# The MLP's up projections as seven products, weights standing and 256 tokens moving, with the norm's weight applied to turned tokens

## The chip, the cores and the metric

One of the eight cores of a Trainium2 chip. The metric is device time of one execution, in microseconds (us). Before the change three runs took 983.56 to 983.86 us, median 983.71.

## What is computed

One layer of a decoder trunk on 512 tokens of 1024 numbers, all in float32. A token mixer (retention and dilated attention, left out here) is added to x, then an MLP, then a gated embedding. The change lies in the MLP's first product and what feeds it and takes from it:

```python
def rmsnorm(x, g):
    y = x * rsqrt(mean(x * x, axis=-1) + EPS)
    return y * g

    x = x + (gate_r * ret_branch + gate_a * att_branch) @ w_o   # w_o: 1024 x 1024
    u = rmsnorm(x, g_mlp) @ w_up                                # w_up: 1024 x 4096
    x = x + square(relu(u)) @ w_down                            # w_down: 4096 x 1024
    gate_p = sigmoid(rmsnorm(x, g_ple) @ w_ple_gate)
    return x + gate_p * (p_i @ w_ple_proj)
```

## The kernel before

**Splits and passes.** TensorE multiplies rounded numbers, so each operand is held as a high part (a rounded copy, by ScalarE, ACT) and a low part (the difference, by VectorE, DVE). A product is three matmul passes into one bank (`mm3`, L256 to L261): high by high, high by low, low by high. A pass has one tile of 128 x 128 standing in TensorE and up to 512 columns moving through it.

**Weights.** They come in units of 512 KB in the order of a plan written ahead. `fetch` has SyncE (SP) load a unit into one of six `raw` tiles; where the plan asks for a sum of two blocks, a second transfer adds to the tile while it lands, issued by GpSimd (POOL, L211 and L225). `ahead` splits units, two or three of them in advance of their use (`AHEAD`); `split_unit` makes the high part on ACT (L247) and the low part on DVE (L248), in one step of 128 x 1024 each, into one of four pairs of tiles (whi, wlo). Where a norm's weight is to be applied, it does so in four steps of 128 x 256 on each engine (L252, L253), the weight of the input channel as a factor.

**Seven products.** `seven_gemm` multiplies 512 x 512 quarters of a matrix by Strassen's scheme in Winograd's form: seven block products instead of eight. The weights' factors are quarters B11, B21, B22 and sums T1 to T4; the left factors are seven blocks of 256 tokens, and each result is added with a sign to one or two quarters of the output (L1120, one step for each half of the tokens and each quarter). `SEVEN` is the order of the products by halves of their inner length. The result banks come from two pools of four; the table `BANK` says which products share one.

**The tail.** `tail` runs, in this order: the output projection (`seven_gemm` on w_o); the embedding product, whose result waits in memory; four groups of the MLP (index f), each an up group (1024 columns of w_up) and a down group (1024 rows of w_down); the gate's product and the sum.

An up group is eight column tiles of `cols_gemm`: weights stand, 512 tokens move, 24 passes a tile. Its input h2 is x turned (tokens to columns) and split by `gain_T`; the norm's weight g_mlp is applied to w_up at the split of its units, and the norm's factor of each token is applied after the MLP's square (f2). `act` takes each finished tile: relu and square on ACT, then, as soon as a pair of quarters is there, `seven_left` builds the differences on DVE and `left_split` the high and low parts of the down group's left factors (L1084 on ACT, L1085 on DVE, up to six blocks of 256 in one step). The down group is a `seven_gemm` that adds into x.

**Order.** Each engine runs its instructions in a fixed order. A scheduler sets it from the program's order and its own estimates; in the stage of the output projection and in the last group's down part, the order on ACT and DVE is the one written in the program (`manual_schedule`), and there `later` and `force` put steps some ticks (a tick is a few matmuls) behind.

Of the kernel before, what the change touches and what calls it, by code (L numbers as in the profile page):

```python
# [11 lines left out]
F32 = mybir.dt.float32  # L12
# [24 lines left out]
FACTOR = {1: "B11", 2: "B21", 3: "B22", 4: "T4", 5: "T1", 6: "T2", 7: "T3"}  # L37
SEVEN_UNITS = [(FACTOR[m], v) for m, u in SEVEN for v in ((0, 1) if u is None else (u,))]
LEFT = {1: 0, 2: 1, 4: 2, 7: 3, 5: 4, 6: 5, 3: 6}
# [41 lines left out]
class Block:  # L81
# [86 lines left out]

    def plan_seven(self, w, r0, c1, c2, vector=False):
# [4 lines left out]
        at = lambda name, u: n + SEVEN_UNITS.index((name, u))  # L174
        for name, u in SEVEN_UNITS:
            if name == "T1":
                src = q(0, 1, u) if vector else (q(0, 1, u), q(0, 0, u))
                if vector:
                    self.added[at("B11", u)] = at("T1", u), at("B11", u)
            elif name == "T4" and vector:  # L180
# [111 lines left out]
    def stat(self, act, k, t, perm):  # L292
        out = []
        for part in act:
            c = part[k // 4][:, k % 4]
            out.append(R(c.rearrange("p (l r) -> p r l", r=DIL)[:, t] if perm else c[:, t * P : (t + 1) * P]))
        return out
# [204 lines left out]
    def embed_load(self):  # L502
        self.pT = self.big("pT")
        self.p_raw = self.big("praw")[:, 0:2]
        self.nc.sync.dma_start(self.p_raw, self.a["p_cols"].rearrange("(k p) t -> p k t", p=P))

    def embed_split(self):
        nc, pT, raw = self.nc, self.pT, self.p_raw
        hi, lo = pT[:, 0:2], pT[:, 2:4]
        nc.scalar.activation(R(hi), raw, AF.Copy)  # L510
        nc.vector.tensor_tensor(R(lo), raw, hi, op=ALU.subtract)

    def embed(self):
        nc = self.nc
        hi, lo = self.pT[:, 0:2], self.pT[:, 2:4]
        self.pp_dram = self.dram.tile([S, D], F32, name="pp_dram", tag="pp_dram")
        for half in range(2):
# [4 lines left out]

            self.rows_gemm(([hi], [lo]), 2, store)

# [561 lines left out]

    def seven_products(self, left, after):

        banks, begun = {}, set()
        for m, half in SEVEN:  # L1090
            us = self.units(2 if half is None else 1)
            for p, u in [(p, u) for p in range(2) for u in ((0, 1) if half is None else (half,))]:
# [3 lines left out]
                wh, wl = us[u if half is None else 0]  # L1096
                for k in range(2):
                    sh, sl = left(m, 2 * u + k, p)
                    self.mm3(banks[b], sh, sl, wh[:, k], wl[:, k], u == 0 and k == 0 and b not in begun,
                             u == 1 and k == 1, b in begun)  # L1100
                if u == 1:
# [3 lines left out]

    def seven_gemm(self, U, xs, f, ready):

        nc = self.nc

        def left(m, kk, p):  # L1110
            c = slice(LEFT[m] * 256 + p * P, LEFT[m] * 256 + (p + 1) * P)
            return (R(U[i][kk].rearrange("p a b -> p (a b)")[:, c]) for i in range(2))

# [9 lines left out]

        self.seven_products(left, after)


    def tail(self, mx):
# [3 lines left out]
        self.embed_load()  # L1131
        h2 = []
        v2 = self.const.tile([P, NT], F32, name="v2")
# [5 lines left out]
        nc.gpsimd.memset(one[:, NT:], -1.0)  # L1139
        left = [2] * NT  # L1140

        def ready(t, j):
            if not h2:
                h2.extend(self.new_act(2, "h2"))
            self.gain_T(xs[t], t, j, h2, "h2", 3)
            left[t] -= 1
            if not left[t]:
                self.mean_squares(xs[t], 7, lambda mean: (mean(v2[:, t : t + 1]), self.done.add(("v2", t))))
            if (t, j) == (3, 0):
                self.embed_split()  # L1150

        with self.tc.manual_schedule(engines={nc.scalar.engine, nc.vector.engine}):
            self.AHEAD = 3
            self.seven_gemm(mx, xs, one, ready)
            self.embed()
            for t in range(NT):
                self.force(("v2", t))
            nc.vector.reciprocal(f2[:, :NT], v2)
            nc.vector.tensor_scalar(f2[:, NT:], f2[:, :NT], -1.0, None, op0=ALU.mult)

        h3 = None
        for f in range(NF // 2):
            U = [[None] * 4, [None] * 4]
            Z = {}

            def act(b, j, ps):
                r = self.tmp("ur")
                nc.scalar.activation(r, ps, AF.Relu)
                if b == 0:
                    z = self.big("z").rearrange("p a (b t) -> p (a b) t", b=2)  # L1170
                    a21 = self.tmp("a21")[:, :256]
                    Z[j] = z, a21
                    nc.scalar.activation(z[:, 0], r[:, :256], AF.Square)
                    nc.scalar.activation(a21, r[:, 256:], AF.Square)
                    self.left_split(z, U, j, 0, 1)
                else:
                    z, a21 = Z[j]
                    nc.scalar.activation(z[:, 1:3], r.rearrange("p (h t) -> p h t", h=2), AF.Square)
                    self.seven_left(z, a21, U, j)
# [23 lines left out]
            self.seven_gemm(U, xs, f2, ready)  # L1203

# [20 lines left out]
    def make_plan(self):  # L1225
# [7 lines left out]
        for c in (0, 512):  # L1233
            self.plan_seven(w, 0, RV + c, RG + c, True)
        self.plan_mix()
        self.plan_seven(a["w_o"][0], 0, 512, 0)
        for half in range(2):
            self.plan_rows(a["w_ple_proj"][0], 512 * half, 2)
        for f in range(NF // 2):
            for jj in range(2):  # L1240
                for b in range(2):
# [46 lines left out]
```

## Time and profile before

| | |
|---|---|
| median of three runs | 983.71 us |
| the profiled execution's own time | 983.3 us |
| its span, first to last instruction | 981.2 us |
| TensorE matmuls (PE), busy | 973.4 us, 99% |
| TensorE weight loads (PEld) | 817.3 us, 83% |
| VectorE (DVE) | 649.7 us, 66% |
| ScalarE (ACT) | 492.5 us, 50% |
| GpSimd (POOL) | 110.8 us, 11% |
| TensorE clock granted | 1.000 of full speed |
| moved by DMA | 136.49 MB |

A row of a timeline gives the start in us from the span's start, the length, the engine, the line, the operation, out<-in by the program's names, and the tile's shape; "x2" at its end means that two instructions were recorded as one row. Matmuls are pipelined, so their recorded lengths overlap: what a pass costs is read from start to start, or from the length of a stretch by its count of passes. A row of busy time by stretch gives the stretch, its length, and then for each engine busy time and count. The table of DMA issues gives queue, count, KB each and the median us from issue to landing. The chain that ended last is followed back from the last instruction, at each step to what released it.

### The profile page before, as it was taken

Reading aid. Unit: us, or ns where it says so; the run is one execution under the profiler, and the core shown is the slowest. Engines: PE = TensorE matmul, PEld = TensorE weight load, DVE = VectorE, ACT = ScalarE, POOL = GpSimd, SP = SyncE. Lnnn points to the kernel's source line nnn. Section 1 sums busy time; section 2 is a strip of 40 time slices with the busy share of each in tenths; the row PEclk is TensorE's granted clock in tenths of the full one; section 3 lists DMA queues with packets and bytes.
Section 4 is the critical chain, followed back from the end, with each engine's and each line's share of the span. In section 5 each row is a group of like instructions: output and inputs, shape, how many; then the busy total and the mean of one; then the engine's idle time right before and its main releaser. Section 6 shows DMA issues by size and latency. Waiting matters only on the chain.

```text
span 981.2 us, 12477 instructions
## 1 busy us (share of the span) xinstructions
PE 973.4 (99%) x4540; PEld 817.3 (83%) x4540; DVE 649.7 (66%) x1029; ACT 492.5 (50%) x1019; POOL 110.8 (11%) x108
## 2 busy tenths in 40 slices
PE   9999999999999999999999999999999999999998
PEld 6888899889888878888888888888888888888886
DVE  7857675775969869464633875677567567667753
ACT  6535344446645547353323457654664564565551
POOL 0310120220001120001001110020001002002000
PEclk9999999999999999999999999999999999999999
DMA  9822123334247744223535676567548548555811
GB/s 333 268 86 88 44 86 86 93 125 140 79 128 186 192 112 143 67 66 108 191 91 127 147 172 215 150 121 203 149 113 209 151 108 183 166 144 119 258 63 53
DMA packets 88508, 136.49 MB, mean 139 GB/s; under 512 B 6096, under 2 KB 40576, under 8 KB 88448
## 3 DMA queue, kind: packets, MB, share of 16 engines
q1 hardware_dynamic: 75248, 110.52, 35.1%
q0 software_dynamic: 13056, 25.17, 15.7%
q8 instruction: 35, 0.57, 0.2%
q14 instruction: 25, 0.20, 0.1%
q10 hardware_dynamic: 144, 0.02, 0.0%
HBM read 131.46 MB, written 4.24 MB: 138 GB/s over the span
## 4 chain that ended last, share of the span: by engine, by line
PE 97%; DVE 1%; POOL 1%; ACT 0%; DMA 0%; issue 0%; SPq 0%; ACTq 0%
PE pg L259 29%; PE pg L261 29%; PE pg L260 29%; PE po L724 1%; PE ph L577 1%; PE pa L261 1%; PE pa L259 1%; PE pa L260 1%; PE pt L335 1%; PE sc L701 1%; PE pe L669 1%; PE kv L972 1%; PE sc L707 1%; PE ry L984 1%; POOL r L325 0%; DVE wlo L248 0%
## 5 line engine op out<-in xcount | busy, mean ns | idle before, releaser
L248 DVE TENSOR_TENSOR wlo<-raw,whi 128x1024 fp32r<-128x1024 f32 (+1 forms) x178 | 210.5, 1190 | 101.7 <-ACT whi L247 100.7
L247 ACT ACTIVATE whi<-raw 128x1024 fp32r<-128x1024 f32 (+1 forms) x177 | 182.2, 1035 | 186.6 <-PE pg L261 99.1
L259 PE MATMUL pg<-whi,hh 128*128 128x512 f32 x344 | 137.8, 402 | 0.0
L261 PE MATMUL pg<-whi,hl 128*128 128x512 f32 x344 | 134.7, 391 | 0.0
L260 PE MATMUL pg<-wlo,hh 128*128 128x512 f32 x344 | 134.5, 391 | 0.0
L259 PE MATMUL pg<-h2h,whi 128*128 128x512 f32 x256 | 99.6, 389 | 0.0
L260 PE MATMUL pg<-h2l,whi 128*128 128x512 f32 x256 | 99.6, 389 | 0.0
L261 PE MATMUL pg<-h2h,wlo 128*128 128x512 f32 x256 | 99.6, 389 | 0.0
L259 PE MATMUL pg<-whi,uh 128*128 128x512 f32 x240 | 94.2, 393 | 0.0
L261 PE MATMUL pg<-whi,ul 128*128 128x512 f32 x240 | 93.4, 390 | 0.0
L260 PE MATMUL pg<-wlo,uh 128*128 128x512 f32 x240 | 93.4, 389 | 0.0
L261 PEld LDWEIGHTS pg<-whi,hl 128*128 128x128 f32 x344 | 72.4, 210 | 11.1
L259 PEld LDWEIGHTS pg<-whi,hh 128*128 128x128 f32 x344 | 72.4, 211 | 10.5 <-ACT whi L247 0.3
L260 PEld LDWEIGHTS pg<-wlo,hh 128*128 128x128 f32 x344 | 72.6, 211 | 10.0
L252 ACT ACTIVATE whi<-raw,gcol 128x256 fp32r<-128x256 f32 (+1 forms) x144 | 65.8, 523 | 30.1 <-PE pg L261 15.4
L253 DVE SCALAR_TENSOR_TENSOR wlo<-raw,gcol,whi 128x256 fp32r<-128x256 f32 (+1 forms) x144 | 66.2, 510 | 21.5 <-ACT whi L252 21.0
L259 PE MATMUL pg<-hh,whi 128*128 128x512 f32 x160 | 64.0, 400 | 0.0
L261 PE MATMUL pg<-hh,wlo 128*128 128x512 f32 x160 | 62.4, 390 | 0.0
L260 PE MATMUL pg<-hl,whi 128*128 128x512 f32 x160 | 62.4, 390 | 0.0
L1085 DVE TENSOR_TENSOR ul<-z,uh 128x256 fp32r<-128x256 f32 (+1 forms) x40 | 43.2, 1090 | 28.3 <-ACT uh L1084 27.7
L260 PEld LDWEIGHTS pg<-h2l,whi 128*128 128x128 f32 x256 | 48.0, 188 | 10.0
L261 PEld LDWEIGHTS pg<-h2h,wlo 128*128 128x128 f32 x256 | 48.0, 188 | 10.0
(222 smaller groups left out, 1760.1 us busy)
## 6 DMA issues: line engine op xcount, KB each, us to landing
raw<-in_w_in SPq DMA_DIRECT2D x72, 512.0 KB, 3.9
raw<-in_w_up SPq DMA_DIRECT2D x32, 512.0 KB, 4.4
raw<-in_w_down SPq DMA_DIRECT2D x32, 512.0 KB, 3.4
raw<-in_w_down POOLq DMA_DIRECT2D x32, 512.0 KB, 5.8
x<-in_x SPq DMA_DIRECT2D x8, 512.0 KB, 6.7
raw<-in_w_in POOLq DMA_DIRECT2D x8, 512.0 KB, 6.4
raw<-in_w_ret_out SPq DMA_DIRECT2D x8, 512.0 KB, 3.6
raw<-in_w_o SPq DMA_DIRECT2D x8, 512.0 KB, 3.3
```

What stands on the lines that cost most here:

```text
L247: self.pin(nc.scalar.activation(R(hi[:, i]), raw[:, i], AF.Copy))
L248: nc.vector.tensor_tensor(R(lo[:, i]), raw[:, i], hi[:, i], op=ALU.subtract)
L252: self.pin(nc.scalar.activation(R(hi[:, i]), raw[:, i], AF.Copy, scale=g))
L253: nc.vector.scalar_tensor_tensor(R(lo[:, i]), raw[:, i], g, hi[:, i], op0=ALU.mult, op1=ALU.subtract)
L259: t.matmul(ps, sh, mh, start=first, stop=False, skip_group_check=more)
L260: t.matmul(ps, sh, ml, start=False, stop=False, skip_group_check=more)
L261: t.matmul(ps, sl, mh, start=False, stop=last, skip_group_check=more)
L335: nc.tensor.transpose(ps[:, k * P : (k + 1) * P], part[:, k * P : (k + 1) * P], self.ident)
L577: self.nc.tensor.transpose(ps[:, t * P : (t + 1) * P], rots[t][:, h * HD : (h + 1) * HD], self.ident)
L669: self.nc.tensor.transpose(ps[:, k * P : (k + 1) * P], e[:, k * P : (k + 1) * P], self.ident)
L701: nc.tensor.matmul(sc[:, h * P : (h + 1) * P], qT[:, h, rs], kT[:, h, rs], start=True, stop=True)
L1085: self.nc.vector.tensor_tensor(R(lo), src, hi, op=ALU.subtract)
```

## The change

Four things change, all in the tail.

1. An up group is computed by `up_products`: seven products here too, with weights standing and 256 tokens moving (`seven_products` with `turned`). For each unit of 256 x 512 weights, four column tiles of 128 by two rows of k by three passes move 256 tokens. The result banks of products 3, 5 and 1, 2 (c and b) are taken at the group's start. The units come from `plan_seven`: T1 by a DVE addition, T2, T3 and T4 by adding transfers.
2. The order of the products is `HALVES` in the up and down groups: both halves of product 1, then both of product 5. The w_o stage keeps `SEVEN`.
3. g_mlp is applied to tokens: `turn` turns a block of x by TensorE and multiplies it by g_mlp on its way out of the bank (DVE), and `quarter` builds the seven left factors of the up groups from it: four differences, seven splits of 128 x 1024.
4. The left factors are tiles by product (`slots`: high and low part of one factor in one tile) in place of tiles by rows of k; the steps that make the down group's factors are in `after`, 512 wide. The embedding's input moves to smaller tiles.

```diff
+HALVES = ((1, 0), (1, 1), (5, 0), (5, 1)) + SEVEN[4:]
...
+    def turn(self, x, out, goff):
+        ps = self.bank("pt")
+        for k in range(4):
+            self.nc.tensor.transpose(ps[:, k * P : (k + 1) * P], x[:, k * P : (k + 1) * P], self.ident)
+        g = self.gcol[:, goff : goff + 4].unsqueeze(2).to_broadcast([P, 4, P])
+        self.nc.vector.tensor_tensor(out, ps.rearrange("p (k t) -> p k t", k=4), g, op=ALU.mult)
...
-    def seven_products(self, left, after):
+    def seven_products(self, left, after, order=SEVEN, turned=False):
         banks, begun = {}, set()
-        for m, half in SEVEN:
+        if turned:
+            banks = {(x, p): self.gbank() for x in "cb" for p in range(2)}
+        for m, half in order:
...
+                for n, k in [(n, k) for n in range(2 if turned else 1) for k in range(2)]:
+                    first, last, more = u == 0 and n == 0 and k == 0 and b not in begun, u == 1 and k == 1, b in begun
+                    if turned:
+                        c = slice(256 * p + P * n, 256 * p + P * (n + 1))
+                        self.mm3(banks[b][:, 256 * n : 256 * (n + 1)], wh[:, k, c], wl[:, k, c], *left(m, 2 * u + k),
+                                 first, last, True)
+                    else:
+                        self.mm3(banks[b], *left(m, 2 * u + k, p), wh[:, k], wl[:, k], first, last, more)
...
+    def slots(self):
+        out = {}
+        def split(m, src, k):
+            if m not in out:
+                out[m] = self.big("f").rearrange("p (s k) (h t) -> p s (k h) t", s=2, h=2)
+            hi, lo = out[m][:, 0, k], out[m][:, 1, k]
+            self.nc.scalar.activation(R(hi), src, AF.Copy)
+            self.nc.vector.tensor_tensor(R(lo), src, hi, op=ALU.subtract)
+        return out, split
...
+        def after(m, p, ps):
+            k = slice(2 * p, 2 * p + 2)
+            if m in (1, 3, 5):
+                held[m, p] = self.tmp("r") if m != 5 else self.tabp.tile([P, 512], F32, tag="tab", name=self.nm("r5"))
+                nc.scalar.activation(held[m, p], ps, AF.Copy)
+                return
+            x = self.tmp("r4") if m == 4 else held[{2: 1, 6: 3, 7: 5}[m], p]
+            if m == 4:
+                nc.scalar.activation(x, ps, AF.Relu)
+            else:
+                nc.vector.tensor_tensor(x, x, ps, op=ALU.add)
+                nc.scalar.activation(x, x, AF.Relu, scale=1.0 if m == 2 else -1.0)
+            nc.scalar.activation(x, x, AF.Square)
+            if m in (2, 6):
+                split({2: 2, 6: 1}[m], v(x), k)
+                return
+            a11, a12, a21 = held[3, p], held[1, p], held[5, p]
+            if m == 7:
+                nc.vector.tensor_tensor(a11, a11, x, op=ALU.subtract)
+                split(7, v(a11), k)
+                return
+            held[4, p] = x
+            nc.vector.tensor_tensor(a21, x, a21, op=ALU.subtract)
+            split(5, v(a21), k)
+            self.differ(a11, x, a11)
+            self.differ(a12, a12, a11)
+            if p:
+                for f, n in ((3, 1), (6, 3), (4, 4)):
+                    for i in range(2):
+                        split(f, v(held[n, i]), slice(2 * i, 2 * i + 2))
...
+        def quarter(i, j):
+            if not i:
+                split(1 + j, zq[0][:, j], every)
+            elif not j:
+                nc.vector.tensor_tensor(a11, a11, a21, op=ALU.subtract)
+                split(7, a11, every)
+            else:
+                nc.vector.tensor_tensor(a21, a22, a21, op=ALU.subtract)
+                split(5, a21, every)
+                self.differ(a11, a22, a11)
+                self.differ(a12, a12, a11)
+                for m, z in ((3, a12), (6, a11), (4, a22)):
+                    self.later(0, lambda m=m, z=z: split(m, z, every), ("h2", m))
...
-            for jj in range(2):
-                for b in range(2):
-                    self.cols_gemm(h2, KD, lambda n, ps: act(b, 2 * jj + n, ps))
+            U = self.up_products(h2)
...
-                    self.plan_cols(a["w_up"][0], 512 * (2 * f + b) + 256 * jj, KD, g0=40)
-            self.plan_seven(a["w_down"][0], 1024 * f, 512, 0)
+            self.plan_seven(a["w_up"][0], 0, 1024 * f + 512, 1024 * f, HALVES, ("T1",))
+            self.plan_seven(a["w_down"][0], 1024 * f, 512, 0, HALVES)
```

The changed file has other line numbers: the split of a unit is L248 (ACT) and L249 (DVE), the three passes L260 to L262, the addition into x L1132, the factors' high and low parts L1146 and L1147, the copies of products 1, 3, 5 L1165, relu and square of products 2, 6, 7 L1172 and L1173 (of product 4, L1169 and L1173).

Three places where the order moves, all in the second group (index 1), from its up group to its down group. First ACT, before the change, from the relu of an up tile to the splits of the down group's first units (ur: relu'd tile; z: squares and differences; uh: high part of left factors; whi: high part of a weight unit):

```order
L1174 ACTIVATE a_6224<-ur_6221 128x256
L1084 ACTIVATE uh_6227<-z_6223 128x256
L1168 ACTIVATE ur_6271<-pg_6231 128x512
L1178 ACTIVATE z_6189<-ur_6271 128x512
L247 ACTIVATE whi_6313<-raw_6311 128x1024
L1084 ACTIVATE uh_6193<-z_6189 128x1536
L247 ACTIVATE whi_6334<-raw_6331 128x1024
L1168 ACTIVATE ur_6303<-pg_6232 128x512
L1178 ACTIVATE z_6223<-ur_6303 128x512
L247 ACTIVATE whi_6355<-raw_6353 128x1024
L1084 ACTIVATE uh_6227<-z_6223 128x1536
L247 ACTIVATE whi_6375<-raw_6373 128x1024
```

ACT after the change, at the end of the up group; ahead of this piece stand the split of T4's first half (whi_6436) and one relu, and its last row is the split of T4's second half (r: a tile of products, taken to relu and square in place; f: a left factor):

```order
L1172 ACTIVATE r_6326<-r_6326 128x512
L1173 ACTIVATE r_6312<-r_6312 128x512
L1173 ACTIVATE r_6326<-r_6326 128x512
L1146 ACTIVATE f_6377<-r_6312 128x512
L1146 ACTIVATE f_6377<-r_6326 128x512
L1172 ACTIVATE r_6152<-r_6152 128x512
L1172 ACTIVATE r_6166<-r_6166 128x512
L1173 ACTIVATE r_6152<-r_6152 128x512
L1173 ACTIVATE r_6166<-r_6166 128x512
L1146 ACTIVATE f_6416<-r_6152 128x512
L1146 ACTIVATE f_6416<-r_6166 128x512
L248 ACTIVATE whi_6440<-raw_6073 128x1024
```

Weight splits stood between any two or three steps of the factors; now twelve steps of the factors (the relu ahead included) stand between two weight splits.

DVE before, at the same hand-over, with the low parts of the down group's third, fourth and fifth units (wlo_6314, wlo_6335, wlo_6356, for products 1, 5 and 2) among the factors' steps:

```order
L248 TENSOR_TENSOR wlo_6314<-raw_6311,whi_6313 128x1024
L1085 TENSOR_TENSOR ul_6194<-z_6189,uh_6193 128x1536
L248 TENSOR_TENSOR wlo_6335<-raw_6331,whi_6334 128x1024
L1072 TENSOR_TENSOR z_6223<-z_6223,a_6224 128x512
L1074 SCALAR_TENSOR_TENSOR z_6223<-z_6223 128x256 x2
L248 TENSOR_TENSOR wlo_6356<-raw_6353,whi_6355 128x1024
L1085 TENSOR_TENSOR ul_6228<-z_6223,uh_6227 128x1536
L1120 SCALAR_TENSOR_TENSOR x_4534<-pg_6317,f_4842,x_4534 128x512
L248 TENSOR_TENSOR wlo_6376<-raw_6373,whi_6375 128x1024
L1120 SCALAR_TENSOR_TENSOR x_4534<-pg_6324,f_4842,x_4534 128x512
```

DVE now, the end of the same stretch; wlo_6644 is the low part of the down group's fifth unit (B21, for product 2):

```order
L1147 TENSOR_TENSOR f_6582<-r_6152,f_6582 128x512
L1147 TENSOR_TENSOR f_6545<-r_6231,f_6545 128x512
L1152 SCALAR_TENSOR_TENSOR r_6166<-r_6166,r_6326 128x512
L1147 TENSOR_TENSOR f_6587<-r_6312,f_6587 128x512
L1147 TENSOR_TENSOR f_6587<-r_6326,f_6587 128x512
L1147 TENSOR_TENSOR f_6582<-r_6166,f_6582 128x512
L1147 TENSOR_TENSOR f_6592<-r_6541,f_6592 128x512
L1147 TENSOR_TENSOR f_6592<-r_6574,f_6592 128x512
L1132 SCALAR_TENSOR_TENSOR x_4534<-pg_6605,f_4843,x_4534 128x512
L1132 SCALAR_TENSOR_TENSOR x_4534<-pg_6612,f_4843,x_4534 128x512
L249 TENSOR_TENSOR wlo_6644<-raw_6641,whi_6643 128x1024
L249 TENSOR_TENSOR wlo_6664<-raw_6661,whi_6663 128x1024
```

The fifth unit's low part now stands behind all the factors' low parts and behind the first two additions into x.

TensorE before, where the down group's product 2 begins (unit 6355 and its low part 6356, bank pa):

```order
L259 MATMUL pa_6401<-whi_6355,uh_6009 128x512
L260 MATMUL pa_6401<-wlo_6356,uh_6009 128x512
L261 MATMUL pa_6401<-whi_6355,ul_6010 128x512
L259 MATMUL pa_6401<-whi_6355,uh_6043 128x512
L260 MATMUL pa_6401<-wlo_6356,uh_6043 128x512
```

TensorE now, at the same place (f_6416 is product 2's left factor, whi_6643 and wlo_6644 its unit; f_6587 and whi_6703 belong to a product with a bank of pool pg):

```order
L260 MATMUL pa_6689<-whi_6643,f_6416 128x512
L260 MATMUL pa_6696<-whi_6643,f_6416 128x512
L260 MATMUL pg_6605<-whi_6703,f_6587 128x512
L260 MATMUL pg_6612<-whi_6703,f_6587 128x512
L261 MATMUL pa_6689<-wlo_6644,f_6416 128x512
L262 MATMUL pa_6689<-whi_6643,f_6416 128x512
```

Four passes that need only high parts now stand ahead of the first that needs the low part wlo_6644; before, the first pass with the low part came second.

More of the change, by code (lines that the diff above doesn't have):

```diff
@@ L173, in plan_seven @@
         n = len(self.plan)
[L174 to L175 removed]
+        units = [(FACTOR[m], v) for m, u in order for v in ((0, 1) if u is None else (u,))]
+        at = lambda name, u: n + units.index((name, u))
+        for name, u in units:
             if name == "T1":
[L177 to L178 removed]
+                src = q(0, 1, u) if name in vector else (q(0, 1, u), q(0, 0, u))
+                if name in vector:
                     self.added[at("B11", u)] = at("T1", u), at("B11", u)
[L180 removed]
+            elif name == "T4" and name in vector:
                 self.added[max(at("B21", u), at("T2", u))] = at("T2", u), at("B21", u)
@@ L1104, in seven_products, with seven_gemm @@
                 self.tick()
-    def seven_gemm(self, U, xs, f, ready):
+    def seven_gemm(self, left, xs, f, ready, order=SEVEN):
         nc = self.nc
-        def left(m, kk, p):
-            c = slice(LEFT[m] * 256 + p * P, LEFT[m] * 256 + (p + 1) * P)
-            return (R(U[i][kk].rearrange("p a b -> p (a b)")[:, c]) for i in range(2))
         def after(m, p, v):
@@ L1122, in after, with differ, up_products @@
                     ready(t, j)
-        self.seven_products(left, after)
+        self.seven_products(left, after, order)
+    def slots(self):
[7 more added lines that the diff above has]
+        return out, split
+    def differ(self, o, x, y):
+        self.nc.vector.scalar_tensor_tensor(o, x, -1.0, y, op0=ALU.mult, op1=ALU.subtract)
+    def up_products(self, h2):
+        nc = self.nc
+        U, split = self.slots()
+        held = {}
+        v = lambda ap: ap.rearrange("p (k t) -> p k t", k=2)
+        def after(m, p, ps):
[28 more added lines that the diff above has]
+                        split(f, v(held[n, i]), slice(2 * i, 2 * i + 2))
+        self.seven_products(lambda m, kk: (R(h2[m][:, 0, kk]), R(h2[m][:, 1, kk])), after, HALVES, True)
+        return U
     def tail(self, mx):
@@ L1140, in tail, with step @@
         left = [2] * NT
-        def ready(t, j):
-            if not h2:
-                h2.extend(self.new_act(2, "h2"))
-            self.gain_T(xs[t], t, j, h2, "h2", 3)
+        h2, split = self.slots()
+        zq = [self.big("zq").rearrange("p (j k) (h t) -> p j (k h) t", j=2, h=2) for _ in range(2)]
+        (a11, a12), (a21, a22) = ([z[:, j] for j in range(2)] for z in zq)
+        every, turned = slice(0, 4), {}
+        def quarter(i, j):
[11 more added lines that the diff above has]
+                    self.later(0, lambda m=m, z=z: split(m, z, every), ("h2", m))
+        def ready(t, j):
+            def step():
+                c = slice(P * (t % 2), P * (t % 2 + 1))
+                self.turn(xs[t][:, 512 * j : 512 * (j + 1)], zq[t // 2][:, j, :, c], 40 + 4 * j)
+                i = t // 2, j
+                turned[i] = turned.get(i, 0) + 1
+                if turned[i] == 2:
+                    self.later(0, lambda: quarter(*i), ("q", i))
+            self.later(3, step)
             left[t] -= 1
@@ L1150, in ready, with mix_left @@
                 self.embed_split()
+        def mix_left(m, kk, p):
+            c = slice(LEFT[m] * 256 + p * P, LEFT[m] * 256 + (p + 1) * P)
+            return (R(mx[i][kk].rearrange("p a b -> p (a b)")[:, c]) for i in range(2))
         with self.tc.manual_schedule(engines={nc.scalar.engine, nc.vector.engine}):
             self.AHEAD = 3
-            self.seven_gemm(mx, xs, one, ready)
+            self.seven_gemm(mix_left, xs, one, ready)
             self.embed()
+            for m in (3, 6, 4):
+                if m == 3:
+                    self.force(("q", (1, 1)))
+                self.force(("h2", m))
             for t in range(NT):
```

54 lines of the change are left out of this document (16 added, 38 removed).

## The prediction

> **What bounds the kernel now.** I read the busy shares first, then the chain that ended last.
>
> ```profile
> PE 973.4 (99%) x4540; PEld 817.3 (83%) x4540; DVE 649.7 (66%) x1029; ACT 492.5 (50%) x1019; POOL 110.8 (11%) x108
> PE 97%; DVE 1%; POOL 1%; ACT 0%; DMA 0%; issue 0%; SPq 0%; ACTq 0%
> ```
>
> TensorE is busy for 99% of the span and is 97% of the chain. Every pass removed shortens the kernel, until another engine makes TensorE wait. Then the busy time by stretch, for the first up group (eight column tiles of `cols_gemm`) and the down group behind it:
>
> ```profile
> 602.25:645.77 43.52, 43.52 (x193) 36.04 (x192) 24.15 (x47) 28.34 (x57) 3.62 (x3) 1.00 0.58 153
> 645.77:683.85 38.08, 38.08 (x169) 31.53 (x168) 30.28 (x39) 18.66 (x25) 6.04 (x5) 1.00 0.76 181
> ```
>
> Columns: length, then busy time and count of PE, PEld, DVE, ACT, POOL, clock, DMA share, GB/s. The up group is 192 passes in 43.52 us, the down group 168 in 38.08: 0.2267 us per 512-wide pass in both, at full clock, with no wait. DVE works 24.2 and 30.3 us, ACT 28.3 and 18.7: there is room on average. What a pass of 256 tokens costs stands at the program's end, where the last column block is halved (timeline of PE, first and last of 48 such passes, and of PEld):
>
> ```profile
> 970.73 0.39 PE L261 MATMUL pg<-whi,h3l 128*128 128x512 f32 x1
> 970.96 0.28 PE L259 MATMUL pg<-whi,h3h 128*128 128x256 f32 x1
> ...
> 976.59 0.28 PE L261 MATMUL pg<-whi,h3l 128*128 128x256 f32 x1
> ```
>
> ```profile
> 970.96 0.19 PEld L260 LDWEIGHTS pg<-wlo,h3h 128*128 128x128 f32 x1
> 971.08 0.19 PEld L261 LDWEIGHTS pg<-whi,h3l 128*128 128x128 f32 x1
> 971.19 0.19 PEld L259 LDWEIGHTS pg<-whi,h3h 128*128 128x128 f32 x1
> ```
>
> (976.59 - 970.96) / 47 = 0.120 us per 256-wide pass, so two of them take 0.240 where one 512-wide takes 0.227. Each load of weights shows 0.19 us and yet one starts every 0.12: loads lie over passes and over each other.
>
> **The change part by part.** *Up products.* An up group was 192 x 0.2267 = 43.5 us. Now it is 7 products x 48 passes (4 rows of k, 4 column tiles, 3 passes) = 336 x 0.120 = 40.3. That is 3.2 us less per group, **-12.8** over four. The 24 passes of a weight unit last 2.88 us. Transposes, down products and gate keep their passes.
>
> [...]
>
> *Weights.* Before, eight units per up group were split in four 256-wide steps; now fourteen units are split in one 1024-wide step on ACT and one on DVE, and two DVE additions make T1. Six units (T2, T3, T4) come by an adding DMA on POOL's queue, as the down group's do.
>
> ```profile
> 736.60 1.40 DVE L1120 SCALAR_TENSOR_TENSOR x<-pg,f,x 128x512 f32<-128x512 f32 x2
> 737.92 1.21 DVE L248 TENSOR_TENSOR wlo<-raw,whi 128x1024 fp32r<-128x1024 f32 x1
> 739.05 0.74 DVE L1120 SCALAR_TENSOR_TENSOR x<-pg,f,x 128x512 f32<-128x512 f32 x1
> ```
>
> ```profile
> 586.03 0.69 DVE L349 TENSOR_TENSOR h2l<-pt,h2h 128x512 fp32r<-128x512 f32 x1
> 586.64 2.35 DVE L248 TENSOR_TENSOR wlo<-raw,whi 128x1024 fp32r<-128x1024 f32 x2
> ```
>
> ```profile
> 578.31 2.00 ACT L247 ACTIVATE whi<-raw 128x1024 fp32r<-128x1024 f32 x2
> 580.20 0.59 ACT L348 ACTIVATE h2h<-pt 128x512 fp32r<-128x512 f32 x1
> ...
> 587.06 0.62 ACT L380 ACTIVATE j<-x 128x512 f32<-128x512 f32 x1
> 587.58 0.19 ACT L380 ACTIVATION_READ_ACCUMULATOR j<-x 128x1 f32 x1
> ```
>
> ```profile
> raw<-in_w_down POOLq DMA_DIRECT2D x32, 512.0 KB, 5.8
> raw<-in_w_up SPq DMA_DIRECT2D x32, 512.0 KB, 4.4
> ```
>
> From start to start in a full queue, DVE takes 0.66 us for an addition into x, 1.13 for a weight split, 0.61 for a 512-wide step; ACT 0.95 and 0.52. Per up group DVE now has 14 x 1.13 + 2 x 1.13 + 28 x 0.61 = 35 us for 40.3 us of passes. Adding DMAs land in 5.8 us, plain loads in 4.4, and each addition has five units (14.4 us) between the split that frees its tile and its own split, so I cost them at nothing; were only one unit left as cover, it would be 5.8 - 2.9 = 2.9 us for one. POOL's queue holds nothing else here.
>
> *The hand-over from up to down.* Here the average does not hold. Count from the group's first pass. Weights have four buffers, so ACT can split T4's first half only when product 6 has used its last unit: 9 x 2.88 = 25.9, plus 0.2 (a 0.28 us pass ends 0.16 after its successor starts). ACT's queue then has that split, twelve 512-wide steps (relu, square, high part of products 6 and 2) and the split of T4's second half: 26.1 + 0.95 + 12 x 0.52 + 0.95 = 34.3. DVE's low part follows, done at 35.5; TensorE needs it at 34.56 + 1.44 = 36.0, no wait. From 34.4 on DVE has no slack: from that low part to the down group's fifth weight split (B21, for product 2) stand 6 weight splits, 19 steps of 512 and 2 additions into x: 6.8 + 11.6 + 1.3 = 19.7 us. With two short waits for ACT's high parts (0.4 by the same counting) it ends at 54.5. TensorE gets there at 40.3 + 48 x 0.2267 = 51.2 and has only four passes that need no low part, to 52.1. So it waits **2.4 us**. Queued behind that split on DVE are the next ones, which TensorE needs 2.7 us later each, and they come every 1.13: one wait per group. In the last group, ordered by hand, the split stands ahead of both additions (1.3 earlier), but only two passes lie ahead (0.45), and the next product then waits for the additions: 1.9. Sum 3 x 2.4 + 1.9 = **+9.1**. If both queues ran 3% quicker or slower than these rows, one wait would be 1.6 or 3.3: 6 to 13 in all. Before, this place held fewer, wider steps, with the splits between them, and TensorE did not wait.
>
> *Entry to the first up group.* The norm's weight moves from weights to tokens. Before, DVE made eight low parts of 512 here; now it applies the weight in eight steps of 512 and then makes four differences and seven low parts of 1024.
>
> ```profile
> 602.25 0.39 PE L259 MATMUL pg<-h2h,whi 128*128 128x512 f32 x1
> ```
>
> Up to here TensorE has the same passes, and the output projection and the embedding hide the first two splits. From 602.2 DVE has eleven 1024-wide steps and small ones in a row (four differences, splits of 7 and 5, five weight units): 12.8 us, to 615.0. ACT then does one weight split and the high parts of factors 3, 6 and 4 and only then copies product 5's first bank: 615.0 + 0.7 + 3 x 0.95 + 0.5 = 619.1. Product 3 writes that bank from 602.25 + 5 x 2.88 + 0.24 = 616.9. Wait **+2.4**, between 1 (a step or two less in the row) and 4 (a weight buffer comes free one unit later).
>
> *Factor tiles by product, HALVES order, banks taken at the start.* The banks that an up group writes first were read long before, so its start is free. The embedding's tiles are smaller: no price.
>
> Sum against the profiled execution's 983.3 (span 981.2, 2.1 around it): 983.3 - 12.8 + 9.1 + 2.4 = 982.0. The median of the runs, 983.71, is 0.4 higher: **982.4**.
>
> **The rivals.** (1) *The hand-over is covered*: 976. DVE's stretch is the longest queue I count, and any step of it in the shade of another, or ACT nearer to 0.48, shortens it; at 0.8 us per hand-over (3.2 for four) and 1 at the entry, 983.7 - 12.8 + 4.2 = 975.1, at 1.2 and 1.5, 977.2. For it: DVE is 79% busy by the sums, not full. Against: the order is fixed, so DVE cannot take the urgent split first.
> (2) *The wait moves forward into product 4*, slower: 989. If ACT's twelve steps each take their whole 0.62 us, as steps that wait on each other do, T4's second half is ready 1.2 later, at 36.7 instead of 35.5, and TensorE stops at 36.0, in mid-group. Product 4 and all behind it come later on both engines: about 4.0 per hand-over, 16 with the last, 3 at the entry: 983.7 - 12.8 + 15.6 + 2.9 = 989.4. It decides from the point where that low part comes after 36.0, a margin of 0.5. For it: that margin. Against: relu, square and split of both halves alternate, so none waits on the step just before it.
> (3) *Standing weights are bound by their loads.* At 0.19 us for each of 1344 loads, 255 us for 174: 1064. [...]
> That the passes are not removed is no case: the order has 336 of 128x256 in each up group.
>
> **How the numbers follow.** Forecast 0.51, rival 1 0.25, rival 2 0.23, rival 3 0.01. The range reaches from 975.0 (most of rival 1) to 989.5 (rival 2's price), which leaves out about 0.2; the forecast's own bounds (waits of 7 to 17 us) are 978 to 988. A difference of 0.2%, 2.0 us, is about what a measurement of this kernel can tell from no change. The forecast is 1.3 below the median, so its 0.51 goes 0.16 to faster, 0.28 to same, 0.07 to slower; rival 1 goes to faster, rival 2 0.03 to same and the rest to slower, as rival 3 does. Faster 0.41, same 0.31, slower 0.28.
>
> **What would show it.** Up groups' passes start every 0.120 us, 40.3 us a group; if 0.19, rival 3. TensorE idle at four places just after a down group's product 5, released by the low part of a weight split, about 2.4 us each; DVE without a gap for some 19 us before. If the idle time stands inside product 4, rival 2; if the four places sum to under 4 us, rival 1. Idle before product 3 of the first up group, released by ACT's copy of product 5. I am wrong in kind if TensorE waits for a DMA, or inside an up group's first nine units from the second on.

## The result, and the profile after

The changed kernel is slower: 994.83 us median (994.44 to 997.01, 4 runs) against 983.63 (983.43 to 983.86, 4 runs) before, ratio 1.0118 (95% interval 1.0101 to 1.0136). The profiled execution took 995.1 us, its span is 993.3.

The page of after, busy time and then the chain that ended last:

```profile
PE 971.0 (98%) x5116; PEld 837.3 (84%) x5116; DVE 694.6 (70%) x1009; ACT 507.4 (51%) x979; POOL 140.0 (14%) x132
PE 22%; DVE 7%; ACT 6%; DMA 2%; issue 1%; DVEq 0%; ACTq 0%
```

TensorE is still busy for 98%, which says little: busy time counts passes at half clock in full (from 659.90 below, 3.20 us busy of 3.20 at clock 0.50). The chain's shares add up to 38% only, so it was not followed to the start; but DVE, ACT and a transfer now stand in it, where TensorE alone had 97%. The busy time by stretch is clearer. After, first up group, then down and up groups in turn (columns as in the prediction; the 0.96 is the granted clock):

```profile
602.48:645.19 42.71, 41.33 (x337) 40.57 (x336) 35.73 (x44) 32.66 (x48) 9.65 (x8) 1.00 0.92 210
645.19:688.93 43.74, 40.92 (x170) 32.48 (x169) 36.30 (x45) 20.60 (x26) 7.26 (x6) 0.96 0.73 172
688.93:729.25 40.32, 40.32 (x338) 40.31 (x336) 25.81 (x29) 27.10 (x39) 9.63 (x8) 1.00 0.93 209
729.25:775.12 45.87, 40.84 (x170) 32.52 (x169) 36.31 (x45) 20.50 (x26) 7.31 (x6) 0.96 0.73 170
775.12:815.43 40.31, 40.31 (x337) 40.30 (x336) 25.80 (x29) 27.09 (x39) 9.65 (x8) 1.00 0.92 200
815.43:860.72 45.29, 40.84 (x170) 32.51 (x169) 36.32 (x45) 20.62 (x26) 7.32 (x6) 0.96 0.74 172
```

From the second on an up group takes 40.3 us, as forecast, and has no wait. The first takes 42.7, 2.4 more, as forecast. The three down groups take 43.7, 45.9 and 45.3 us where each took 38.1: 20.7 us are lost there. The last down part with what follows takes 1.6 more (901.03 to 993.3, against 890.57 to 981.2). With 0.2 ahead of the first up group, the spans' difference is accounted for: -0.8 - 3 x 3.2 + 20.7 + 1.6 + 0.2 = 12.1.

What TensorE waited for in these three pairs of groups (us in total, times, longest), and one row of the same view for DVE:

```profile
PE pg L260 <- DVE x L1132: 8.3, 3, 3.7
PE pg L260 <- ACT whi L248: 2.1, 3, 0.7
PE pa L261 <- DVE wlo L249: 1.9, 3, 0.6
```

```profile
DVE raw L224 <- DMA raw<-in_w_up: 12.4, 3, 5.0
```

The last two PE rows are the hand-over: TensorE meets a high part that ACT has not made yet, and then the low part, which ends the wait. Timeline of TensorE there, second group:

```profile
740.15 0.61 PE L260 MATMUL pa<-whi,f 128*128 128x512 f32 x2
741.47 0.98 PE L260 MATMUL pg<-whi,f 128*128 128x512 f32 x2 [0.70 <-ACT whi L248]
743.09 0.50 PE L261 MATMUL pa<-wlo,f 128*128 128x512 f32 x1 [0.64 <-DVE wlo L249]
```

Four passes from 740.15 would be done with their turn at 741.06; the first pass with the low part starts at 743.09, so 2.0 us are lost, and that in each of the three. The first PE row of the waits, the largest, was in no forecast. TensorE and DVE near the end of that down group:

```profile
763.89 0.39 PE L262 MATMUL pg<-whi,f 128*128 128x512 f32 x1
767.97 0.47 PE L260 MATMUL pg<-whi,f 128*128 128x512 f32 x1 [3.70 <-DVE x L1132]
```

```profile
755.96 1.41 DVE L1132 SCALAR_TENSOR_TENSOR x<-pg,f,x 128x512 f32<-128x512 f32 x2
762.35 1.23 DVE L224 TENSOR_TENSOR raw<-raw,raw 128x1024 f32<-128x1024 f32 x1 [4.99 <-DMA raw<-in_w_up]
763.49 1.40 DVE L1132 SCALAR_TENSOR_TENSOR x<-pa,f,x 128x512 f32<-128x512 f32 x2
764.81 2.35 DVE L249 TENSOR_TENSOR wlo<-raw,whi 128x1024 fp32r<-128x1024 f32 x2
767.08 0.74 DVE L1132 SCALAR_TENSOR_TENSOR x<-pg,f,x 128x512 f32<-128x512 f32 x1
```

DVE stands idle for 5 us at the addition that makes T1 of the *next* up group (L224), because one summand has not landed. Behind it in DVE's queue are the reads of product 2's banks, T4's two low parts and the read of product 7's bank; TensorE needs that bank for product 4 at 764.1 and gets it at 767.8. An instruction for the next stage blocks the reads of this one. Start to start the three waits are 0.16 longer than idle time shows (a pass's recorded end lies that far behind its successor's start): 8.3 + 0.5 = 8.8 us.

The T1 load came late. Issues in POOL's and then SP's queue:

```profile
744.54 1.20 POOL L226 DMA_DIRECT2D raw<-in_w_down  x1 [9.48 <-DVE wlo L249]
746.99 3.68 POOL L226 DMA_DIRECT2D raw<-in_w_down  x3 [1.25 <-DVE wlo L249]
```

```profile
753.51 0.37 SPq L210 DMA_DIRECT2D raw<-in_w_up  x1
```

Each adding transfer is released by a low part (wlo); behind the hand-over these come in a row, so four adding transfers are issued within some 6 us (744.54 to 750.67), and the T1 load issued at 753.51 lands only at 762.2.

The rest is TensorE's clock. Stretches of after, the first one spanning the first group's hand-over:

```profile
656.20:659.90 3.70, 2.38 (x9) 1.21 (x8) 3.70 (x5) 1.06 (x1) 0.00 (x0) 1.00 0.00 0
659.90:663.10 3.20, 3.20 (x9) 2.50 (x8) 3.20 (x5) 0.10 (x1) 1.39 (x2) 0.50 0.85 188
769.20:772.60 3.40, 3.40 (x9) 2.63 (x8) 2.83 (x4) 0.00 (x0) 0.00 (x0) 0.51 0.74 237
854.50:857.90 3.40, 3.40 (x10) 2.60 (x9) 2.98 (x4) 0.00 (x0) 0.00 (x0) 0.50 0.74 225
```

Once in each of these down groups TensorE ran at half clock for 3.2 to 3.4 us: in the first behind the hand-over's wait of 2.0 us, in the other two behind the waits of 3.9 and 3.3 us for the blocked reads. With 20.7 lost in all, 8.8 in the blocked reads and 6.1 at the hand-overs (3 x 2.03), 5.8 is left, 5.0 of it these 10 us at half clock; the other 0.8 is not assigned.

### The profile page after: what moved, and what is told of

It reads as the page before. It is cut to its first block, busy times and chain, and to the rows that moved or that the text cites. A ratio compares the mean times of both kernels' runs of the same rounds, so it can differ in the third digit from the quotient of the medians.

```text
span 993.3 us, 13654 instructions
## 1 busy us (share of the span) xinstructions
PE 971.0 (98%) x5116; PEld 837.3 (84%) x5116; DVE 694.6 (70%) x1009; ACT 507.4 (51%) x979; POOL 140.0 (14%) x132
## 5 line engine op out<-in xcount | busy, mean ns | idle before, releaser
L249 DVE TENSOR_TENSOR wlo<-raw,whi 128x1024 fp32r<-128x1024 f32 (+1 forms) x234 | 277.9, 1197 | 134.4 <-ACT whi L248 129.8
L248 ACT ACTIVATE whi<-raw 128x1024 fp32r<-128x1024 f32 (+1 forms) x233 | 240.9, 1039 | 249.8 <-PE pg L262 103.8
L260 PE MATMUL pg<-whi,hh 128*128 128x512 f32 x344 | 137.8, 402 | 0.0
L262 PE MATMUL pg<-whi,hl 128*128 128x512 f32 x344 | 134.7, 391 | 0.0
L260 PE MATMUL pg<-f,whi 128*128 128x256 f32 x384 | 108.6, 284 | 1.0 <-ACT r L1165 0.9
L261 PE MATMUL pg<-f,whi 128*128 128x256 f32 x384 | 108.6, 283 | 0.4 <-DVE f L1147 0.4
L262 PE MATMUL pg<-f,wlo 128*128 128x256 f32 x384 | 108.5, 283 | 0.0
L260 PE MATMUL pg<-whi,f 128*128 128x512 f32 x192 | 77.6, 406 | 10.5 <-DVE x L1132 8.3
L262 PEld LDWEIGHTS pg<-whi,hl 128*128 128x128 f32 x344 | 72.4, 210 | 11.1
L260 PEld LDWEIGHTS pg<-whi,hh 128*128 128x128 f32 x344 | 72.4, 211 | 10.5 <-ACT whi L248 0.3
L261 PE MATMUL pg<-wlo,f 128*128 128x512 f32 x192 | 76.2, 397 | 0.0
L262 PE MATMUL pg<-whi,f 128*128 128x512 f32 x192 | 76.1, 397 | 0.0
L260 PEld LDWEIGHTS pg<-f,whi 128*128 128x128 f32 x384 | 73.5, 192 | 1.6 <-ACT r L1165 1.1
L261 PEld LDWEIGHTS pg<-f,whi 128*128 128x128 f32 x384 | 73.7, 192 | 0.8 <-DVE f L1147 0.6
L262 PEld LDWEIGHTS pg<-f,wlo 128*128 128x128 f32 x384 | 73.7, 192 | 0.0
L260 PE MATMUL pg<-hh,whi 128*128 128x512 f32 x160 | 64.0, 400 | 0.0
L262 PE MATMUL pg<-hh,wlo 128*128 128x512 f32 x160 | 62.4, 390 | 0.0
L260 PEld LDWEIGHTS pg<-whi,f 128*128 128x128 f32 x192 | 37.0, 193 | 21.9 <-issue 7.8
L642 POOL TENSOR_TENSOR r<-v,mhalf 128x4 f32<-128x4 f32 x24 | 30.0, 1252 | 153.6 <-DVE v L641 150.7
```

Source lines behind the costliest of these rows:

```text
L248: self.pin(nc.scalar.activation(R(hi[:, i]), raw[:, i], AF.Copy))
L249: nc.vector.tensor_tensor(R(lo[:, i]), raw[:, i], hi[:, i], op=ALU.subtract)
L260: t.matmul(ps, sh, mh, start=first, stop=False, skip_group_check=more)
L261: t.matmul(ps, sh, ml, start=False, stop=False, skip_group_check=more)
L262: t.matmul(ps, sl, mh, start=False, stop=last, skip_group_check=more)
L642: nc.gpsimd.tensor_tensor(r, v, self.mhalf[:, :H], op=ALU.pow)
```

## The experiments

Theory A: the unforeseen loss comes from the T1 addition's place in DVE's queue. Theory B: it comes from the transfers that the hand-over bunches; T4 and T1 arrive late, and TensorE would wait there wherever the addition stood. The first four runs tell these apart; they were measured against 983.94 before.

**T1 summed by a transfer.**

```diff
-            self.plan_seven(a["w_up"][0], 0, 1024 * f + 512, 1024 * f, HALVES, ("T1",))
+            self.plan_seven(a["w_up"][0], 0, 1024 * f + 512, 1024 * f, HALVES)
```

> T1 of the up groups is summed by an adding transfer, as T2 to T4 are, and no longer by DVE. Theory A (blocked queue): in groups 1 to 3 DVE stands at the addition for the next up group's T1 until its load lands, the reads of the banks of products 2 and 7 stand behind it, and TensorE waits for those reads (1.7, 3.9 and 3.3 us in the profile after); its clock is then at half for some 3.3 us, 1.6 us each time. Without the addition these 8.8 us and the two half-clock stretches behind the long waits go: 995.1 - 8.8 - 3.2 = 983. Theory B (late transfers): four adding transfers issued within 5 us after the hand-over come in one after another, T4's last one with them, so TensorE waits there whatever DVE does; two more adding transfers a group make it no better: 990 to 995.

Measured: 983.83 us (982.12 to 985.84, 10 runs), ratio 0.9996 (0.9986 to 1.0005). Theory A's number. The down groups, first and second:

```profile
645.32:686.42 41.10, 39.20 (x171) 31.38 (x169) 34.15 (x43) 20.61 (x26) 9.70 (x8) 1.00 0.83 185
726.73:767.63 40.90, 39.23 (x171) 31.38 (x169) 34.08 (x42) 19.96 (x26) 9.72 (x8) 1.00 0.84 187
```

41.1 and 40.9 us at whole clock: the hand-over's 2.0 are still there, and 0.5 to 1.0 at the place of the blocked reads, which is what B could claim at most. There DVE's queue stands for 1.4 us at the low part of one of T4's units (760.03, second group), whose split on ACT waits 2.9 us for its adding transfer, and a read of a result bank stands behind it: B's late transfer, at a much smaller price.

**T1 without its second summand.**

```diff
-                if name in vector:
+                if name in vector and "bare" not in vector:
                     self.added[at("B11", u)] = at("T1", u), at("B11", u)
...
-            self.plan_seven(a["w_up"][0], 0, 1024 * f + 512, 1024 * f, HALVES, ("T1",))
+            self.plan_seven(a["w_up"][0], 0, 1024 * f + 512, 1024 * f, HALVES, ("T1", "bare"))
```

> Leaves out the second summand of T1 in the up groups: T1's tile holds one block alone, so neither DVE nor a transfer adds to it; all else as in the change. Theory A: 983, as with the sum by transfer; the difference between the two is the price of two more adding transfers a group. Theory B: the transfers of T4 come as late as before, 989 or more.

Measured: 984.85 us (983.62 to 988.26, 10 runs), ratio 1.0007 (0.9993 to 1.0020). The three down groups take 41.9 us each: the hand-over's 2.0 and a stretch at half clock behind it (clock 0.96 over the group), no wait for the reads. As A expected. What the two added transfers a group of the run above cost cannot be read from the two medians, since the clock differs (0.998 to 1.000 over the executions there, 0.995 to 1.000 here); without them TensorE has no wait for the reads, where that run had 1.7 us in the three groups.

**Written order, the addition kept on DVE.**

```diff
-            if f == NF // 2 - 1:
+            if True:
                 order = self.tc.manual_schedule(engines={nc.scalar.engine, nc.vector.engine})
                 order.__enter__()
-                self.AHEAD = 3
+                self.AHEAD = 3 if f == NF // 2 - 1 else 2
...
+            if f < NF // 2 - 1:
+                order.__exit__(None, None, None)
```

> Down parts of all four groups in written order on ACT and DVE, as the last group's was; the addition for the next T1 stays on DVE, but stands six rows later in its queue, behind the reads of products 2 and 7. The hand-over's order is the same. Theory A: the reads are no longer blocked, 983 to 985. Theory B: nothing about the transfers changes, 992 to 995.

Measured: 983.05 us (980.78 to 985.66, 10 runs), ratio 0.9988 (0.9978 to 0.9999). This is the sharpest of the four: as many instructions run on each engine as in the change, and only the order on ACT and DVE in the down parts differs. (That order moves some weight splits too, not only the addition.) TensorE has no wait for the reads. The DVE timeline, second group, shows the addition behind the read of product 7's bank, with nothing to wait for:

```profile
763.96 0.75 DVE L1132 SCALAR_TENSOR_TENSOR x<-pg,f,x 128x512 f32<-128x512 f32 x1 [1.76 <-PE pg L262]
764.63 1.22 DVE L249 TENSOR_TENSOR wlo<-raw,whi 128x1024 fp32r<-128x1024 f32 x1
765.76 1.22 DVE L224 TENSOR_TENSOR raw<-raw,raw 128x1024 f32<-128x1024 f32 x1
```

Theory A holds: with the addition behind the reads the profiled execution is 9.4 us shorter (985.66 against 995.1), and both of these hold three stretches at half clock; the medians differ by 11.8. The hand-over is unchanged, 2.0 us in each group.

**Factors 6 and 4 behind the first down products.**

```diff
+LATE = {6: 1, 4: 5}
...
         def after(m, p, v):
             self.AHEAD = 2
+            if p and late is not None and ("late", m) in late:
+                late[("late", m)]()
...
                 for f, n in ((3, 1), (6, 3), (4, 4)):
-                    for i in range(2):
-                        split(f, v(held[n, i]), slice(2 * i, 2 * i + 2))
+                    def late(f=f, n=n):
+                        for i in range(2):
+                            split(f, v(held[n, i]), slice(2 * i, 2 * i + 2))
+                    if f in LATE:
+                        U["late", LATE[f]] = late
+                    else:
+                        late()
```

> The high and low parts of the down group's factors 6 and 4 (eight steps of 512 a group) are written behind products 1 and 5 of the down group, so two steps fewer stand ahead of the fifth unit's low part on DVE. T1 as in the change. Theory A: the hand-over's wait shrinks by 1.2 us in each group, and the second wait by as much since the loads start earlier: 995.1 - 3 x 2.4 = 988. Theory B: the hand-over sets off the pile of transfers, so the second wait falls with it: 995.1 - 3 x (1.2 + 3.5) = 981.

Measured: 983.01 us (981.94 to 987.17, 10 runs), ratio 0.9993 (0.9979 to 1.0007), between the two expectations. TensorE's waits from 600 to 905 us:

```profile
PE pg L261 <- DVE x L1135: 3.4, 3, 1.9
PE pg L261 <- ACT whi L249: 3.3, 4, 1.2
```

The wait for the fifth unit's low part is gone, but not the hand-over: there TensorE now waits for ACT's split of another unit alone (the second row), 0.7 idle and 0.86 start to start in each group, where it lost 2.0. That is the 1.2 that both theories gave. The wait for the reads fell from 8.3 to 3.4 although the addition kept its place, but at the same place of the first group, the start of product 4, TensorE now waits 1.2 us for a split on ACT (680.20, in the second row too). With that, 1.2, 1.3 and 1.9 us are left there, 4.5 of 8.3: 3.8 went, about A's 3.6, and no share of B is needed. That the run is 5 us below A's 988 is the clock, of which A took no account: no stretch at half clock here (granted clock 1.00 over each of the three groups), where the change lost 5.0 us to them.

The next four were measured against 983.49 before, and ask what the parts are worth together.

**Down parts freed of both.** Written order as above, on TensorE too, and

```diff
+LATE = {3: 1, 6: 5, 4: 3}
...
-        self.ahead(n + (0 if self.pinned else self.AHEAD))
+        self.ahead(n if self.pinned else min(n + self.AHEAD, 4))
...
-            self.AHEAD = 2
+            if late is None:
+                self.AHEAD = 2
...
-                self.AHEAD = 3
+                self.AHEAD = 3 if f == NF // 2 - 1 else 3
```

with the late factors now written behind the additions into x.

> Down parts in written order on ACT, DVE and TensorE; the parts of the down group's factors 3, 6 and 4 written behind products 1, 5 and 3 of the down group; weight splits of the down parts one unit further ahead, so that the fifth unit's low part stands ahead of the first additions into x. T1 stays a DVE addition. If the waits at the hand-over and the blocked reads are all that the down groups lost (theory A with the forecast's hand-over), each takes 38.1 us again, the clock stays whole, and the entry's 2.4 and 0.2 remain: 983.3 - 12.8 + 2.6 = 973. If late transfers hold T4 back (theory B), 1 to 2 us remain in each of three groups: 977 to 980.

Measured: 976.77 us (976.46 to 978.61, 4 runs), ratio 0.9935 (0.9920 to 0.9950), 3.8 above the 973 and at the edge of the range given for late transfers. The trace says that it is not they: each down group takes 39.0 to 39.2 us; TensorE waits 0.8 (start to start) for the read of product 5's bank (DVE L1134) ahead of product 3, four times, and nowhere for T4. The clock is whole (1.000 in all four executions), and the hand-over has no wait left.

**The entry's order alone.**

```diff
-            for m in (3, 6, 4):
-                if m == 3:
-                    self.force(("q", (1, 1)))
-                self.force(("h2", m))
+            self.force(("q", (1, 1)))
+            self.force(("h2", 3))
...
                 nc.scalar.activation(held[m, p], ps, AF.Copy)
+                if m == 5 and p and rest is not None:
+                    rest()
                 return
```

(`rest` splits h2's factors 6 and 4, in the first group.)

> One part alone: of the up groups' own factors, 6 and 4 are split behind ACT's copies of product 5's banks and no longer ahead of them; all else as in the change. By the forecast's account of the entry, the 1.1 us that TensorE waits for ACT's copy go and the 0.6 at the low part of factor 5 stays: the first up group takes 41.4 us (42.7 before), the whole 1.3 less than the change, 993.5. If the copy only hides a later wait, 995.

Measured: 994.93 us (992.57 to 996.52, 4 runs), ratio 1.0121 (1.0104 to 1.0138). The first up group takes 41.92 us, 0.8 less than in the change: ACT's copy no longer holds TensorE, but the low part of factor 3 does, for 0.6. So the copy hid a later wait, and removing it gave back 0.8 of the 2.4 us at the entry, not the 1.3 expected. In the median 0.8 us are lost among the clock's stretches (0.994 to 0.995 over an execution): inconclusive there, clear in the group.

**Both.**

> The kernel with down parts in written order, late factors and earlier splits, and the entry's order as well. If the parts add up: 973 - 1.3 = 972. If late transfers hold: 976 to 979.

Measured: 975.97 us (975.32 to 976.64, 4 runs), ratio 0.9923 (0.9908 to 0.9938): 0.8 less than without the entry's order, as the group above said.

**Both, T1 summed by a transfer.**

> The same, with T1 of the up groups summed by an adding transfer in place of DVE. Theory A: DVE's queue is no longer blocked either way, the same within 1 us, 972. Theory B: two more adding transfers on one queue delay T4 and T1: 975 to 980.

Measured: 975.50 us (975.15 to 975.80, 4 runs), ratio 0.9918 (0.9903 to 0.9933). The same within 1 us of the run above, as A expected. The number itself also lies in B's range, 975 to 980, but only because the run that it builds on came out at 975.97 and not at 972.

The last two were measured against 983.84 before.

**Passes that fill the wait.** Written order as in the third run, with TensorE too, and

```diff
+            if not turned and order is HALVES and (m, half) == (2, 0):
+                spare, (sh, _) = self.bank("fill"), left(2, 0, 0)
+                for i in range(9):
+                    self.nc.tensor.matmul(spare, sh, self.filler, start=True, stop=True)
```

> Down parts in written order on ACT, DVE and TensorE, and nine passes of 512 whose result is not used (9 x 0.227 = 2.0 us) ahead of the down group's product 2, where TensorE would wait 2.1 us. They add work and take nothing away. If TensorE's half clock behind the hand-over (3.3 us long in each of three groups of the run with written order, 1.6 us lost each time) follows from its waiting, the clock stays at 1.0 and a down group takes 38.1 + 2.0 + some 0.5 = 40.6 where that run had 41.9: 979. If the half clock comes whether TensorE waits there or not, 41.9 and 983 or more.

Measured: 983.84 us (982.98 to 984.49, 10 runs), ratio 0.9997 (0.9988 to 1.0007). First down group of the run with written order, and then of this one:

```profile
645.12:686.99 41.87, 40.55 (x170) 32.63 (x169) 35.71 (x44) 20.62 (x26) 7.26 (x6) 0.96 0.74 168
```

```profile
645.28:686.25 40.97, 40.46 (x180) 33.16 (x178) 35.73 (x44) 20.63 (x26) 7.30 (x6) 1.00 0.77 177
```

With 2.0 us of useless work a group is 0.9 shorter, and the clock is 0.999 or 1.000 in all ten executions, where the run with written order had 0.995 to 0.998 in nine of ten, and 980.78 us, its fastest, in the one with 1.000. That fits a clock that follows TensorE's waiting, but does not show it: this run also has TensorE in written order, which the run that it is compared with has not, and no run has that order without the filler and with the wait. The run with T1 by a transfer kept its clock at 0.998 or more with the whole wait. The total missed 979: the last group pays for its filler too, 0.7 us of wait stay in each group, and the 983.05 that it was counted from already holds executions with fewer stretches at half clock than the profiled one.

**Splits further ahead for product 1 only.** The version with T1 by a transfer, and

```diff
-            if late is None:
+            if late is None or m == 1:
                 self.AHEAD = 2
```

> The version with T1 by adding transfer, late factors, written order and the entry's order, with the further-ahead weight splits for product 1 only: from product 5 on splits go two units ahead again, so one split (1.13 us) leaves DVE's stretch ahead of the reads of product 5's banks, for which TensorE still waits 0.8 us in each down group. If DVE's queue is all that this wait hangs on, it goes: 975.5 - 4 x 0.8 = 972.3. If another step takes its place, 975.

Measured: 972.26 us (972.03 to 972.79, 4 runs), ratio 0.9877 (0.9861 to 0.9894), as expected. The down groups take what they took before the change, with no wait:

```profile
645.06:683.18 38.12, 38.12 (x170) 31.54 (x169) 33.95 (x42) 19.63 (x25) 9.70 (x8) 1.00 0.88 198
723.50:761.60 38.10, 38.10 (x170) 31.54 (x169) 33.94 (x42) 19.63 (x25) 9.72 (x8) 1.00 0.87 201
```

By the medians it beats both kernels: 11.6 us faster than before the change, and 22.6 faster than the change as made, which was measured at another time. That is the 12.8 of the passes less 1.6 at the entry, within 0.4.

## Why the prediction was wrong

Forecast 982.0 against the profiled execution, measured 995.1.

- **Up products, -12.8: right.** 40.3 us a group, a pass every 0.120, no wait inside.
- **Hand-over, +9.1: right in place and kind, slightly large.** 2.0 us in three groups and 1.6 in the last, 7.7. The 1.6 is all that the last down part and what follows lost; the profile shows 1.0 of it as the wait for the low part. The wait ends on the low part that was named, and freeing DVE's queue ahead of it removed that. A second wait lay under it that the working does not have, 0.86 a group for ACT's high part of another unit; it showed once the first was gone, and the runs with TensorE in written order do not have it.
- **Entry, +2.4: right in size, half right in cause.** 2.4 measured. That the two agree is partly luck: the working's own times, 619.1 and 616.9, give 2.2. ACT's copy of product 5 was half of it at most, and without it 0.8 went; TensorE waits for the low part of factor 5 before it, and for that of factor 3 once the copy is out of the way.
- **Rivals 1 to 3 did not happen.** The hand-over was not covered, product 4 of the up groups did not stop, and loads of weights are not the limit: a pass every 0.120 us, with each load recorded at 0.19.
- **The step that failed** is the sentence on the weights: "each addition has five units (14.4 us) between the split that frees its tile and its own split, so I cost them at nothing", with the two DVE additions for T1 counted only as 2 x 1.13 us of DVE's time. The working followed the transfers that POOL adds and DVE's total, and did not ask where the T1 addition stands in DVE's queue. It stands in the down group ahead of the reads of the banks of products 2 and 7, and it waits for a load of the next stage. Price: 8.8 us. Moving it behind those reads, taking it off DVE, or leaving it out each removed that wait, wholly or to under 1 us a group. This waiting for a DMA, one step removed, was what the prediction called wrong in kind.
- **A second term was missing altogether:** the stretches at half clock that stand behind three of the waits. They took 5.0 us more, and 0.8 lost in the down groups stays unassigned; the sum below has both as 5.8. Ahead of one of them TensorE did not stand idle throughout: the stretch from 659.90 follows 3.7 us in which it was busy for 2.38.
- 8.8 + 5.8 - 1.4 (hand-over) + 0.2 (ahead of the up groups) - 0.3 (less around the span) = 13.1, the whole difference.

Two things stay open. Why the T1 load took 8.7 us was only argued (adding transfers beside it); no run changed the transfers alone. And TensorE waits at the hand-over as long with T1 by a transfer, whose clock is 0.998 or more in all ten executions, as in the run with written order, whose clock is 0.998 or less in nine of ten: so waits as long were followed by half clock in some executions and not in others.

The traces narrow the second. In the change and with written order each stretch at half clock is 3.41 us long in the record of the clock, and in each of the two runs their starts lie whole multiples of 3.41 us apart: 659.92, 769.15 and 854.48 in the change (32 and 25 times), 659.63, 741.55 and 823.47 with written order (24 times each). So each trace can be cut into windows of 3.41 us that are counted from these starts. The second group's hand-over lies in one window with written order, and is divided between two with T1 by a transfer (cut there from the end of full clock, 982.07):

```profile
738.14:741.55 3.41, 2.08 (x8) 0.96 (x7) 3.41 (x5) 1.20 (x2) 0.00 (x0) 1.00 0.00 0
741.55:744.96 3.41, 3.41 (x10) 2.64 (x9) 3.41 (x5) 0.00 (x0) 1.20 (x1) 0.50 0.64 168
```

```profile
736.31:739.72 3.41, 2.72 (x11) 1.66 (x9) 3.41 (x6) 2.46 (x3) 0.00 (x0) 1.00 0.01 2
739.72:743.13 3.41, 2.77 (x12) 2.14 (x12) 3.41 (x5) 0.00 (x0) 1.11 (x1) 1.00 0.40 101
```

In the MLP's groups of all profiles, the window ahead of each stretch at half clock had TensorE busy for 0.91 to 2.09 us, and no window with more led to one; with filler passes the windows at the hand-over had 2.90 and more. So in these traces the clock behind a wait went with where the wait fell against the windows, and not with its length alone. That does not settle it: six windows with 1.48 to 2.09 us busy, behind which the clock stayed whole, stand against it (two each in the change, in the run with late factors 6 and 4 and in the run with the entry's order alone).

## What to carry to other kernels

For each new step on an engine that reads result banks, ask what it waits for and which reads are queued behind it; an operation for the next stage that waits for a load belongs behind the last read of this one. Busy shares (DVE 70%) and totals per group don't show this. Behind waits of TensorE of 2.0, 3.3 and 3.9 us the clock took up to 1.7 us more here (3.41 us at 0.50), though not behind each wait of 2.0: allow for as much. Where a faster stage moves the loss to its neighbours, look there: the 12.8 us were real, and 11.6 of them came out once the order of the three queues, the late factors and the splits were set for them.

## What the runs showed of the hardware that was not expected

Half clock (0.50) for 3.4 us followed a wait of TensorE of only 2.0 us in the first group of the change, and the clock stayed whole behind waits as long in the first two down groups with T1 by a transfer (1.00 over each). With useless passes in the wait the clock stayed at 0.999 to 1.000 in ten executions, though the passes alone were not shown to be the cause. A load of 512 KB of w_up, which has a median of 4.6 us to landing over 32 such loads, took 8.7 while adding transfers were under way (issued at 753.51; the four issued from 744.54 to 750.67 have a median of 8.2).
